# Stores on GpSimd's queue and a fourth staging tile in the wide part of a one-core decoder layer

## The chip, the cores and the metric

The kernel runs on one core of one Trainium2 chip. The metric is the device time of one execution in microseconds (us). A difference below 0.3%, about 6 us, can't be told from none with this kernel.

## The reference

One layer of a hybrid decoder on 1024 tokens of width 2048, all in float32. What matters here are its three large matrix products and what stands between them:

```python
h = rmsnorm(h_res, g_pre)
u = h @ w_in                      # 2048 x 7184: q, k, v, branch gates of both head groups
o_gla = rmsnorm(gla_chunked(...), g_gla_head) * silu(g_gate)
o_sb = stick_breaking(...) * silu(s_gate)
mix = concat([o_gla, o_sb]) @ w_out              # 2048 x 2048
h_res = h_res + rmsnorm(mix, g_post)
gate = sigmoid(h_res @ w_ple_gate + b_ple_gate)  # 2048 x 2048
out = h_res + gate * (p @ w_ple_proj)
```

## The kernel before

Everything is kept transposed: a tile has 128 features as its partitions and tokens along the free dimension. A wide tile is `[128, 1024]` float32, 512 KB, and holds two feature blocks for 512 tokens.

A float32 product is made of three matmuls in the rounded type fp32r. Each operand is split into a rounded part `hi` (an activation that copies, on ScalarE) and the rest `lo` (a subtraction on VectorE), both in `split`, L110. Then hi\*hi, lo\*hi and hi\*lo are added in PSUM. `product` (L866) does so for one column block of a weight and eight blocks of an activation: 24 matmuls of 128x512.

The first part (up to L807) is the projection `w_in` with the attention of both head groups beside it. The wide part, which the change touches, begins at L810. It computes the branch gates (`w_gate`, which are columns of `w_in`), `w_out` and `w_g`, each as a 2 x 2 block product with seven products instead of eight (Winograd's form). So each has a loop over eight columns j in which three quarters of the weight, `b11`, `t1` and `t2`, are loaded, subtracted from one another on VectorE and split, and two products are made per column: `S2` times `w2` and `S1` times `w1` (L1001 for the gates, L1062 for `w_out`, L1233 for `w_g`). In the first two, both `t2` and `b11` are stored to DRAM for later loops (`t2_d` and `t3_d`, which the trace calls `g_d`); in the third only `t2` is (`u_d`). The other loops load one or two weights per column.

What sets the order of the work:

- The tile framework's scheduler turns the program into one fixed order per engine, and a semaphore wait holds everything that stands behind it on that engine. `dma` and `dma2` (L65, L66) are both SP's `dma_start`, so all loads and stores of the kernel stand in SP's one order and go to one hardware queue.
- Weights are loaded into the four `wr` tiles (`wload2`, L853). A `wr` tile is free again when it is split, and, if it is stored, when the store has landed. Their splits go to three pairs `wh`, `wl`.
- Activations and intermediate results are loaded into three staging tiles `ar` (`staged`, L835). Jobs that run beside the loops (`fill`, `sums_12`, `stream`, `gates_11`) take these in turn, and make the split sets of activations for a later loop.
- `sums_12` (L909) is the job on which the first part of the prediction rests. For each of four blocks i it loads two blocks of `og_d` (the gated attention output) into staging tiles a and b, computes a = a + b and b = A11 - a, stores b to `s2_d` (in the trace `s_d`) and splits both. Its results are the sets `S1` and `S2` of the `w_out` loop with three weights (L1062). It runs beside the loop before that (L1051).
- Results are made in four wide tiles `ev`, in `st_u` and `st_v` (`st`), and for the last four columns of the first small products in two narrow tiles `cw` of `[128, 512]` (L818), each stored to `c11_d`.
- `to_slot` and `act_wide` hold the split activations (`ah`, `al`).

```python
def staged(src):
    t = mt("ar", 3)
    dma2(t, src)
    return t
```

GpSimd works in the first part only (sums of squares, masks, memsets).

Of the kernel before, what the change touches and what calls it, by code (L numbers as in the profile page):

```python
# [21 lines left out]
HT = 512  # L22
# [38 lines left out]
def layer(ctx, tc, xT, w_in, w_gate, w_lr, w_a2, b_a, g_pre, g_head, w_out, g_post,  # L61
          w_g, b_g, w_p, pT, ident, masks, sel_in, out):
    nc = tc.nc
    V, A, G, PE = nc.vector, nc.scalar, nc.gpsimd, nc.tensor
    dma = nc.sync.dma_start  # L65
    dma2 = nc.sync.dma_start  # L66
# [69 lines left out]
    def part(t, k):  # L136
        return t[:, (k % 2) * HT:(k % 2 + 1) * HT]
# [70 lines left out]
    x_act = {hf: [None] * KT for hf in HALVES}  # L208
# [59 lines left out]
    og_d = [[dram.tile([P, W], F32, name=f"og_d{n}_{hf}") for n in range(KP)] for hf in HALVES]  # L268

    keep = ctx.enter_context(tc.tile_pool(name="keep", bufs=1, reuse_waits="tile"))  # L270
    with tc.tile_pool(name="att", bufs=1, reuse_waits="tile") as ap:
# [483 lines left out]
        def small_product(a, src, evac):  # L755
            p = ps("dn")
            for q in range(2):
                hi, lo = wload(part(src, q))
                for kk in range(4):
                    k = 4 * q + kk  # L760
                    sl = slice(kk * P, (kk + 1) * P)
                    ah, al = a[k]
                    mm(p, hi[:, sl], ah, k == 0, False)
                    mm(p, lo[:, sl], ah, False, False)
                    mm(p, hi[:, sl], al, False, k == 7)
                    if k % 2:
                        step()
            with tc.high_priority(offset=300):
                evac(p)
# [15 lines left out]
        def keep_11(j, new):  # L785
            def go(p):
                t = new()
                V.tensor_tensor(t, p, part(u1_s[j // 2], j) if j < 6 else u1_s[j], op=ALU.add)
                dma2(part(c11_d[j // 2], j), t)
            return go  # L790
# [18 lines left out]

    mp = ctx.enter_context(tc.tile_pool(name="mix", bufs=1, reuse_waits="tile"))  # L810
    late = [None]

    def mt(tag, bufs, n=W, dt=F32, name=None):
        pool = keep if tag == "ar" else mp if tag in ("wr", "wh", "wl", "cw") else late[0]
        return pool.tile([P, n], dt, tag=tag, name=nm(name or tag), bufs=bufs)

    for j in order_11[8 - LAST_11:]:
        small_product(x_act[0][8:], w_gate[1, 0, j], keep_11(j, lambda: mt("cw", 2, HT)))  # L818
    w_open.__exit__(None, None, None)
    late[0] = ctx.enter_context(tc.tile_pool(name="late", bufs=1, reuse_waits="tile", side="right"))  # L820
    if True:
# [8 lines left out]
        def to_slot(s, i, raw):  # L830
            pair = act_wide(*slots[s][i])
            split(*pair, raw)
            return pair

        def staged(src):  # L835
            t = mt("ar", 3)
            dma2(t, src)
            return t

# [40 lines left out]
        st_u, st_v = state("h"), state("l")  # L880
# [28 lines left out]
        def sums_12():  # L909
            s1, s2 = [], []  # L910
            for i in range(4):
                a, b = staged(og_d[1][i]), staged(og_d[1][i + 4])
                add(a, a, b)
                hi, lo = sets["A11 pairs"][i]
                add(b, f(hi), f(lo))
                sub(b, b, a)
                dma2(s2_d[i], b)
                yield 1
                s2.append(to_slot(1, i, b))
                yield 1  # L920
                s1.append(to_slot(2, i, a))
                yield 1
            sets["S1"], sets["S2"] = parts(s1), parts(s2)
# [3 lines left out]
        m_d, s2_d, t2_d, t3_d = drams("m_d", 4), drams("s2_d", 4), drams("t2_d", 8), drams("t3_d", 8)  # L927
        c_d = [drams(f"c{hf}_d", KP) for hf in HALVES]
        h_d = [drams(f"h{hf}_d", KP) for hf in HALVES]
# [30 lines left out]
        def stream(hf, kp, c):  # L960
            x = staged(xT[hf, kp])
            for n in (2 * kp, 2 * kp + 1):
                V.scalar_tensor_tensor(part(c, n), part(c, n), gpost_s[:, n:n + 1], r[hf],
                                       op0=ALU.mult, op1=ALU.mult)
            add(c, c, x)
            dma2(h_d[hf][kp], c)
            yield 1


        wide = {}  # L970
# [12 lines left out]
        def finish(z, hf, kp):  # L983
            o, g = staged(o_d[hf][kp]), mt("sq", 1)
            z3 = z.rearrange("p (a t) -> p a t", a=2)
            V.tensor_tensor(z3, z3, rstd[hf].rearrange("p (o t) -> p o t", o=1).to_broadcast([P, 2, HT]),
                            op=ALU.mult)
            A.activation(g, z, AF.Sigmoid)
            V.tensor_tensor(z, z, o, op=ALU.mult)
            V.tensor_tensor(z, z, g, op=ALU.mult)  # L990
            dma2(og_d[hf][kp], z)

        def gates_11():
            for i in range(4):
# [4 lines left out]
        t2_d, t3_d = drams("g2_d", 8), drams("g3_d", 8)  # L999
        dma2(st_u[3], u1_d)  # L1000
        for j in range(8):  # L1001
            with ahead():
                b11, t1, t2 = (wload2(w_gate[kh, nh, j]) for kh, nh in ((0, 0), (0, 1), (1, 1)))
                sub(t1, t1, b11)
                sub(t2, t1, t2)
                w2, w1 = wsplit(t2), wsplit(t1)
                add(b11, b11, t2)
                dma2(t2_d[j], t2)
                dma2(t3_d[j], b11)
            p = product(g_sets["S2"], w2)  # L1010
            with soon():
                add(u(j), p, part(u1_s[j // 2], j) if j < 6 else u(j))
            p = product(g_sets["S1"], w1)
            with soon():
                add(v(j), p, u(j))
# [30 lines left out]
        st_u, st_v = state("h"), state("l")  # L1046
# [4 lines left out]
        for j in range(8):  # L1051
            with ahead():
                w = wsplit(wload2(w_out[0, 0, j]))
            p = product(sets["A11"], w)
            with soon():
                A.activation(u(j), p, AF.Copy)
                if j % 2:
                    dma2(m_d[j // 2], st_u[j // 2])
        drain()

        job(fill("S3", 0, both(og_d[1], og_d[0], sub)))
        for j in range(8):  # L1062
            with ahead():
                b11, t1, t2 = (wload2(w_out[kh, nh, j]) for kh, nh in ((0, 0), (0, 1), (1, 1)))
                sub(t1, t1, b11)
                sub(t2, t1, t2)
                w2, w1 = wsplit(t2), wsplit(t1)
                add(b11, b11, t2)
                dma2(t2_d[j], t2)
                dma2(t3_d[j], b11)  # L1070
            p = product(sets["S2"], w2)
            with soon():
                add(u(j), p, u(j))
            p = product(sets["S1"], w1)
            with soon():
                add(v(j), p, u(j))
# [4 lines left out]
        for j in range(8):  # L1081
            with ahead():
                w = wsplit(wload2(t3_d[j]))
            p = product(sets["S3"], w)
            with soon():
                if j % 2 == 0:
                    c = mt("ev", 4)
                add(part(c, j), p, v(j))
                add(u(j), p, u(j))
                if j % 2:  # L1090
                    dma2(c_d[1][4 + j // 2], c)
                    squares(1, c)
        drain()

# [25 lines left out]
        for j in range(8):  # L1120
            with ahead():
                w = wsplit(wload2(w_out[1, 0, j]))
            p = product(sets["A12"], w)
            with soon():
                if j % 2 == 0:
                    c = staged(m_d[j // 2])
                add(part(c, j), p, part(c, j))
                if j % 2:
                    dma2(c_d[0][j // 2], c)
                    squares(0, c)  # L1130
        drain()

# [38 lines left out]
        def gated(n, hf, p, other, last=False):  # L1171
            key = n // 8, hf
            if n % 2 == 0:
                wide[key] = mt("ev", 4)
                res[key] = staged(h_d[hf][n // 2])
            t, h = part(wide[key], n), res[key]
            add(t, p, other)
            g = mt("g", 1, HT)
            A.activation(g, t, AF.Sigmoid, bias=bg_s[:, n:n + 1])
            V.tensor_tensor(t, pw.pop((n, hf)), g, op=ALU.mult)  # L1180
            if last:
                add(t, t, part(h, n))
                dma2(part(out[hf, n // 2], n), t)
            elif n % 2:
                add(wide[key], wide[key], h)
                dma2(out[hf, n // 2], wide[key])

        def stream_0():
            norm(0)
# [43 lines left out]
        for j in range(8):  # L1233
            with ahead():
                b11, t1, t2 = (wload2(w_g[kh, nh, j]) for kh, nh in ((0, 0), (0, 1), (1, 1)))
                sub(t1, t1, b11)
                sub(t2, t1, t2)
                w2, w1 = wsplit(t2), wsplit(t1)
                dma2(t2_d[j], t2)
            p = product(sets["S2"], w2)  # L1240
            with soon():
                add(u(j), p, u(j))
            p = product(sets["S1"], w1)
            with soon():
                add(v(j), p, u(j))
# [99 lines left out]
```

## Time and profile before

| | us |
|---|---|
| median of three runs | 2112.08 |
| their range | 2111.71 to 2118.36 |
| the profiled execution | 2116.28 |
| its span, first to last instruction | 2114.6 |
| TensorE busy | 2078.6 (98%) |
| VectorE busy | 1502.2 (71%) |
| ScalarE busy | 873.9 (41%) |
| GpSimd busy | 106.6 (5%) |

In this profile a row of instructions names the source line, the engine, the operation and the tiles as out<-in. PE is TensorE, DVE is VectorE, ACT is ScalarE, POOL is GpSimd, SP is SyncE, and SPq is its queue, which issues the transfers. In a timeline row the first two numbers are the start and the duration in us; square brackets give the idle time before it and what ended that. The chain of waits has the same two numbers and then what filled the time. A landing is the time from the issue of a transfer to the semaphore that tells of its end. Matmuls are pipelined, so that the busy time of TensorE hides short losses.

### The profile page before, as it was taken

Reading aid. Unit: us, or ns where it says so; the run is one execution under the profiler, and the core shown is the slowest. Engines: PE = TensorE matmul, PEld = TensorE weight load, DVE = VectorE, ACT = ScalarE, POOL = GpSimd, SP = SyncE. Lnnn points to the kernel's source line nnn. Section 1 sums busy time; section 2 is a strip of 40 time slices with the busy share of each in tenths; the row PEclk is TensorE's granted clock in tenths of the full one; section 3 lists DMA queues with packets and bytes.
Section 4 is the critical chain, followed back from the end, with each engine's and each line's share of the span. In section 5 each row is a group of like instructions: output and inputs, shape, how many; then the busy total and the mean of one; then the engine's idle time right before and its main releaser. Section 6 shows DMA issues by size and latency. Waiting matters only on the chain.

```text
span 2114.6 us, 26802 instructions
## 1 busy us (share of the span) xinstructions
PE 2078.6 (98%) x9712; PEld 1709.8 (81%) x9712; DVE 1502.2 (71%) x2259; ACT 873.9 (41%) x1389; POOL 106.6 (5%) x228
## 2 busy tenths in 40 slices
PE   9999999999999999999999999999899999999998
PEld 6788888888887888888888787788688888777887
DVE  8557767676766676666567667897777787876665
ACT  7333433343455455545456313333233444423332
POOL 3000000000011011101101000000000000000000
PEclk9999999999999999999999999999899999999999
DMA  6222222222344344433335787887887685777763
GB/s 210 68 70 77 80 75 83 70 85 65 78 107 106 94 103 119 105 94 101 76 95 153 236 291 279 295 274 276 301 299 249 214 311 200 273 273 232 237 200 122
DMA packets 229812, 352.81 MB, mean 167 GB/s; under 512 B 124464, under 2 KB 129456, under 8 KB 229680
## 3 DMA queue, kind: packets, MB, share of 16 engines
q1 hardware_dynamic: 229680, 351.11, 52.7%
q8 instruction: 76, 1.25, 0.2%
q14 instruction: 56, 0.46, 0.1%
HBM read 249.85 MB, written 73.92 MB: 153 GB/s over the span
## 4 chain that ended last, share of the span: by engine, by line
PE 61%; DMA 16%; DVE 15%; issue 4%; ACT 3%; SPq 0%; POOL 0%; DVEq 0%; ACTq 0%; POOLq 0%
PE dn L100 52%; PE z L100 4%; DMA wr<-w_g 4%; DVE wl L112 3%; PE o L100 2%; PE t L100 2%; DMA wr<-w_gate 2%; DVE wr L848 1%; DMA E<-X 1%; DMA ar<-h_d 1%; DVE wr L851 1%; DVE ev L848 1%; DVE al L112 1%; DMA ar<-og_d 1%; DMA g_d<-wr 1%
## 5 line engine op out<-in xcount | busy, mean ns | idle before, releaser
L100 PE MATMUL dn<-ah,hi 128*128 128x512 f32 x1408 | 562.7, 400 | 2.0 <-ACT hi L111 1.3
L100 PE MATMUL dn<-al,hi 128*128 128x512 f32 x1408 | 550.7, 391 | 1.0 <-DVE al L241 1.0
L100 PE MATMUL dn<-ah,lo 128*128 128x512 f32 x1408 | 550.4, 391 | 0.2 <-DVE lo L112 0.2
L100 PE MATMUL dn<-ah,wh 128*128 128x512 f32 x1216 | 476.0, 391 | 7.8 <-ACT ah L111 5.5
L100 PE MATMUL dn<-ah,wl 128*128 128x512 f32 x1216 | 476.7, 392 | 5.4 <-DVE wl L112 5.3
L100 PE MATMUL dn<-al,wh 128*128 128x512 f32 x1216 | 474.9, 391 | 0.1
L100 PEld LDWEIGHTS dn<-ah,hi 128*128 128x128 f32 x1408 | 265.7, 189 | 61.5 <-ACT ah L240 4.2
L100 PEld LDWEIGHTS dn<-al,hi 128*128 128x128 f32 x1408 | 264.7, 188 | 59.9 <-DVE al L241 2.5
L100 PEld LDWEIGHTS dn<-ah,lo 128*128 128x128 f32 x1408 | 265.7, 189 | 48.3 <-DVE lo L112 0.5
L100 PEld LDWEIGHTS dn<-ah,wl 128*128 128x128 f32 x1216 | 229.4, 189 | 58.7 <-DVE wl L112 11.4
L100 PEld LDWEIGHTS dn<-ah,wh 128*128 128x128 f32 x1216 | 229.5, 189 | 57.9 <-ACT ah L111 6.5
L100 PEld LDWEIGHTS dn<-al,wh 128*128 128x128 f32 x1216 | 229.2, 188 | 47.9 <-DVE al L112 0.8
L111 ACT ACTIVATE wh<-wr 128x1024 fp32r<-128x1024 f32 x152 | 158.5, 1054 | 252.5 <-DVE wr L851 133.1
L112 DVE TENSOR_TENSOR wl<-wr,wh 128x1024 fp32r<-128x1024 f32 x152 | 184.9, 1218 | 6.4 <-ACT wh L111 6.0
L111 ACT ACTIVATE hi<-raw 128x512 fp32r<-128x512 f32 x192 | 120.1, 626 | 142.1 <-PE dn L100 136.3
L112 DVE TENSOR_TENSOR lo<-raw,hi 128x512 fp32r<-128x512 f32 x192 | 133.6, 697 | 57.9 <-ACT hi L111 57.5
L324 ACT ACTIVATE X<-E 128x256 uint16<-128x256 uint16 (+2 forms) x96 | 81.0, 843 | 127.0 <-DVE E L599 118.3
L594 DVE TENSOR_TENSOR_SCAN X<-X 128x128 f32<-128x128 f32 (+2 forms) x96 | 98.1, 1022 | 31.5 <-POOL X L588 21.6
L111 ACT ACTIVATE ah<-ar 128x1024 fp32r<-128x1024 f32 x56 | 59.2, 1060 | 121.3 <-DVE ar L848 63.8
L609 DVE COPY v<-E 128x512 uint16<-128x512 uint16 (+1 forms) x160 | 63.5, 428 | 55.1 <-DMA E<-X 45.7
L851 DVE TENSOR_TENSOR wr<-wr,wr 128x1024 f32<-128x1024 f32 x48 | 58.7, 1223 | 57.3 <-DMA wr<-w_gate 18.0
L848 DVE TENSOR_TENSOR wr<-wr,wr 128x1024 f32<-128x1024 f32 x48 | 58.8, 1224 | 50.9 <-DMA wr<-w_g 32.2
(233 smaller groups left out, 2305.7 us busy)
## 6 DMA issues: line engine op xcount, KB each, us to landing
raw<-w_in SPq DMA_DIRECT2D x160, 256.0 KB, 2.7
wr<-w_g SPq DMA_DIRECT2D x64, 512.0 KB, 4.3
wr<-w_out SPq DMA_DIRECT2D x56, 512.0 KB, 4.7
wr<-w_gate SPq DMA_DIRECT2D x40, 512.0 KB, 5.1
ar<-h_d SPq DMA_DIRECT2D x36, 512.0 KB, 4.9
g_d<-wr SPq DMA_DIRECT2D x32, 512.0 KB, 2.8
wr<-g_d SPq DMA_DIRECT2D x32, 512.0 KB, 4.6
ar<-og_d SPq DMA_DIRECT2D x32, 512.0 KB, 5.0
```

Of the source, the lines that this page charges most:

```text
L100: PE.matmul(o, lhsT, rhs, start=start, stop=stop)
L111: A.activation(hi, src, AF.Copy)
L112: (eng or V).tensor_tensor(lo, src, f(hi), op=ALU.subtract)
L324: A.activation(pl.rearrange("p (two n) -> p two n", two=2), src.bitcast(U16)[:, :2 * n].rearrange("p (n two) -> p two n", two=2), AF.Copy)
L594: V.tensor_tensor_scan(rev, rev, rev, initial=kq[:, n:n + 1], op0=ALU.mult, op1=ALU.bypass)
L609: V.tensor_copy(to[:, :, :m, j], w[:, :, 2 * g:2 * g + m])
L848: V.tensor_tensor(dst, a, b, op=ALU.add)
L851: V.tensor_tensor(dst, a, b, op=ALU.subtract)
```

## The change

All stores from the wide part on go through a new name, `store`, which is GpSimd's `dma_start`, except the last narrow ones to `out` (L1183). Loads stay on SP. The staging tiles become four: every fourth call of `staged` takes the wide tile `cw` in place of an `ar`. For that, the two narrow `cw` tiles of `[128, 512]` become one of `[128, 1024]`, which takes the results of columns j and j + 1 in its halves. The space for descriptors of transfers that GpSimd issues is doubled.

```diff
+    store = G.dma_start
...
+    cw = {}
+
+    def at_cw(j):
+        if j % 2 == 0:
+            cw[0] = mt("cw", 1)
+        return part(cw[0], j)
+
     for j in order_11[8 - LAST_11:]:
-        small_product(x_act[0][8:], w_gate[1, 0, j], keep_11(j, lambda: mt("cw", 2, HT)))
+        small_product(x_act[0][8:], w_gate[1, 0, j], keep_11(j, lambda: at_cw(j)))
...
+        spare = itertools.cycle((("ar", 3), ("ar", 3), ("ar", 3), ("cw", 1)))
+
         def staged(src):
-            t = mt("ar", 3)
+            t = mt(*next(spare))
             dma2(t, src)
             return t
...
-                dma2(s2_d[i], b)
+                store(s2_d[i], b)
...
-            dma2(h_d[hf][kp], c)
+            store(h_d[hf][kp], c)
...
-            dma2(og_d[hf][kp], z)
+            store(og_d[hf][kp], z)
...
-                dma2(t2_d[j], t2)
-                dma2(t3_d[j], b11)
+                store(t2_d[j], t2)
+                store(t3_d[j], b11)
...
-                    dma2(m_d[j // 2], st_u[j // 2])
+                    store(m_d[j // 2], st_u[j // 2])
...
-                    dma2(c_d[0][j // 2], c)
+                    store(c_d[0][j // 2], c)
...
-                dma2(out[hf, n // 2], wide[key])
+                store(out[hf, n // 2], wide[key])
...
-                   dynamic_dma_scratch_size=1024)
+                   dynamic_dma_scratch_size=2048)
```

The pair of stores of `t2` and `b11` occurs in the loops for the gates and for `w_out`, the one of `t2` alone in that for `w_g`; `c_d[1]` is stored in the same way as `c_d[0]`. Together 103 stores move from SP to GpSimd. The scheduler then orders anew. Up to the wide part no order changes.

**SP where the `w_out` loop with three weights begins.** In the program before, the loads for the fourth block of `sums_12` are the two of `og_d_1_712` and `og_d_1_716`. The names `wr` with numbers from 13627 on are the weights of the second and third column, and `g_d` and `m_d` are stores:

```order
L855 DMA wr_13698<-w_out 128x1024
L1069 DMA g_d_11584<-wr_13631 128x1024
L1070 DMA g_d_11592<-wr_13627 128x1024
L1058 DMA m_d_11530<-st_13191 128x1024
L855 DMA wr_13700<-w_out 128x1024
L855 DMA wr_13702<-w_out 128x1024
L837 DMA ar_13325<-og_d_1_712 128x1024
L837 DMA ar_13327<-og_d_1_716 128x1024
```

Now, still on SP, `wr_13518`, `wr_13520` and `wr_13522` are `b11`, `t1` and `t2` of the first column:

```order
L847 DMA ar_13282<-og_d_1_715 128x1024
L865 DMA wr_13518<-w_out 128x1024
L847 DMA ar_13323<-og_d_1_712 128x1024
L865 DMA wr_13520<-w_out 128x1024
L847 DMA cw_13325<-og_d_1_716 128x1024
L847 DMA ar_13541<-og_d_1_709 128x1024
L865 DMA wr_13522<-w_out 128x1024
```

The two loads have moved from behind the stores of the second column to between the weight loads of the first; one of them goes to `cw`, and no store stands among them. On VectorE the sums and splits of the fourth block, which stood behind the weights of the third column, now end next to the split of the first column's `t2`.

**TensorE at the same place.** In the program before, the first product with `S2` is `dn_13539`, and the first with `S1` is `dn_13583`:

```order
L100 MATMUL dn_13539<-ah_13296,wh_13528 128x512
L100 MATMUL dn_13539<-ah_13296,wl_13529 128x512
L100 MATMUL dn_13539<-al_13297,wh_13528 128x512
L100 MATMUL dn_13583<-ah_13230,wh_13532 128x512
L100 MATMUL dn_13583<-ah_13230,wl_13533 128x512
L100 MATMUL dn_13583<-al_13231,wh_13532 128x512
```

Now the product with `S2` is `dn_13537`, and `ah_13337` is its fourth pair:

```order
L100 MATMUL dn_13537<-ah_13294,wh_13526 128x512
L100 MATMUL dn_13537<-ah_13294,wl_13527 128x512
L100 MATMUL dn_13537<-al_13295,wh_13526 128x512
L100 MATMUL dn_13537<-ah_13337,wh_13526 128x512
L100 MATMUL dn_13537<-ah_13337,wl_13527 128x512
L100 MATMUL dn_13537<-al_13338,wh_13526 128x512
```

Before, TensorE left the product after its third pair, with 18 of 24 matmuls done, and began the next two in the same way; now each product runs through.

**SP and GpSimd in the gates' loop with three weights.** Before, on SP, with what each waits for (`DMAHWn` is one of eight semaphores that SP's transfers use in turn), one column:

```order
L1008 DMA g_d_11586<-wr_11817 128x1024 [waits DVE_49]
L1009 DMA g_d_11594<-wr_11813 128x1024 [waits DVE_49]
L855 DMA wr_11886<-w_gate 128x1024 [waits DMAHW6_49,DVE_49]
L855 DMA wr_11888<-w_gate 128x1024 [waits DMAHW1_49,DVE_49]
L855 DMA wr_11955<-w_gate 128x1024 [waits DMAHW7_49,DMAHW2_49]
```

Now the loads on SP (`DMASWn` are the eight semaphores of GpSimd's stores, in turn from 0), and a column's two stores on POOL:

```order
L865 DMA wr_11884<-w_gate 128x1024 [waits DMAHW1_49,DMASW6_49,DVE_49]
L865 DMA wr_11886<-w_gate 128x1024 [waits DMAHW2_49,DVE_49]
L865 DMA wr_11953<-w_gate 128x1024 [waits DMAHW3_49,DMASW7_49]
L865 DMA wr_11955<-w_gate 128x1024 [waits DMAHW4_49,DMASW0_49,DVE_49]
L847 DMA ar_12197<-S3x_d_748 128x1024 [waits DMAHW5_49,DVE_49]
L865 DMA wr_11957<-w_gate 128x1024 [waits DMAHW6_49,DMASW1_49]
```

```order
L1018 DMA g_d_11584<-wr_11815 128x1024 [waits DVE_49]
L1019 DMA g_d_11592<-wr_11811 128x1024 [waits DVE_49]
L1018 DMA g_d_11585<-wr_11886 128x1024 [waits DMASW0_49,DVE_49]
L1019 DMA g_d_11593<-wr_11882 128x1024 [waits DMASW1_49,DVE_49]
```

The stores have left SP's order, and its loads wait in place of them for the landing of the stores that GpSimd issues (`DMASW6` is that of `wr_11815`, `DMASW7` that of `wr_11811`).

More of the change, by code (lines that the diff above doesn't have):

```diff
@@ L1068, in layer @@
                 add(b11, b11, t2)
-                dma2(t2_d[j], t2)
-                dma2(t3_d[j], b11)
+                store(t2_d[j], t2)
+                store(t3_d[j], b11)
             p = product(sets["S2"], w2)
@@ L1090, in layer @@
                 if j % 2:
-                    dma2(c_d[1][4 + j // 2], c)
+                    store(c_d[1][4 + j // 2], c)
                     squares(1, c)
@@ L1238, in layer @@
                 w2, w1 = wsplit(t2), wsplit(t1)
-                dma2(t2_d[j], t2)
+                store(t2_d[j], t2)
             p = product(sets["S2"], w2)
```

## The prediction

> **What bounds the kernel now.** The page first:
>
> ```profile
> span 2114.6 us, 26802 instructions
> ...
> PE 2078.6 (98%) x9712; PEld 1709.8 (81%) x9712; DVE 1502.2 (71%) x2259; ACT 873.9 (41%) x1389; POOL 106.6 (5%) x228
> ```
>
> TensorE is the bound. But its busy time counts a matmul as 0.39 us although the next one starts sooner, so a busy share of 98% does not say how much is lost. The chain of waits gives the true pace, from a run with nothing in between:
>
> ```profile
> 1668.38 81.62 PE dn L100 x360
> ```
>
> 81.62 / 360 = 0.2267 us a matmul. A product of 24 therefore takes 5.44 us, and a column of two products 10.88. With this pace the table by stage (busy time and count of each engine, granted clock, DMA share, GB/s) tells what the wide part loses:
>
> ```profile
> 1208.00:1480.00 272.00, 270.92 (x1187) 221.64 (x1186) 214.10 (x210) 86.34 (x90) 0.00 (x0) 1.00 0.81 283
> 1480.00:1504.00 24.00, 15.38 (x40) 10.05 (x39) 13.69 (x12) 4.60 (x5) 0.00 (x0) 0.72 0.89 319
> 1504.00:1860.00 356.00, 354.39 (x1558) 291.51 (x1557) 278.88 (x298) 138.45 (x147) 0.00 (x0) 1.00 0.75 260
> 1860.00:1940.00 80.00, 76.43 (x333) 61.55 (x332) 59.37 (x60) 20.98 (x21) 0.00 (x0) 1.00 0.75 253
> ```
>
> Count times 0.2267, taken from the length: 2.9, 14.9, 2.8 and 4.5 us lost. So of some 25 us, 14.9 lie in 24 us, where the granted clock also falls to 0.72. All that this change can win lies in these four numbers; before 1195 us nothing moves. The waits of TensorE there:
>
> ```profile
> 1481.82 0.50 PE L100 MATMUL dn<-ah,wh 128*128 128x512 f32 x1 [1.05 <-ACT wh L111]
> ...
> 1494.20 0.80 PE L100 MATMUL dn<-ah,wh 128*128 128x512 f32 x1 [5.38 <-ACT ah L111]
> 1498.78 0.80 PE L100 MATMUL dn<-ah,wh 128*128 128x512 f32 x1 [1.21 <-ACT wh L111]
> ```
>
> The longest wait is for `ah`, a split activation: the last pair that `sums_12` makes. Followed back in the timeline:
>
> ```profile
> 1491.83 1.23 DVE L848 TENSOR_TENSOR ar<-ar,ar 128x1024 f32<-128x1024 f32 x1
> ...
> 1493.09 1.06 ACT L111 ACTIVATE ah<-ar 128x1024 fp32r<-128x1024 f32 x1 [10.84 <-DVE ar L848]
> ```
>
> The first sum of that pair starts only at 1491.83. SP's queue shows why its two staged loads are so late:
>
> ```profile
> 1480.62 0.33 SPq L1069 DMA_DIRECT2D g_d<-wr  x1
> 1481.88 0.33 SPq L1070 DMA_DIRECT2D g_d<-wr  x1
> 1482.28 0.43 SPq L1058 DMA_DIRECT2D m_d<-st  x1
> 1483.27 1.57 SPq L855 DMA_DIRECT2D wr<-w_out  x2
> 1484.88 0.94 SPq L837 DMA_DIRECT2D ar<-og_d  x2
> ```
>
> The two `ar` loads leave at 1484.88, behind three stores that had waited for their data and two weight loads queued behind these. Over the whole wide part SP waited for stores as follows (us in total, times, longest):
>
> ```profile
> SPq L1008 <- DVE wr L851: 42.5, 8, 6.0
> ...
> SPq L1069 <- DVE wr L851: 26.2, 8, 5.8
> ```
>
> **The change part by part.** *Stores to GpSimd.* 103 transfers leave SP. GpSimd is busy for 0.00 us in the table, so nothing stands in front of them there, and a store that waits for its data now holds up only other stores. What it costs is the landing. The trace shows no transfer issued by GpSimd, so I bound it by stores of SP (size, median us from issue to landing):
>
> ```profile
> g_d<-wr SPq DMA_DIRECT2D x32, 512.0 KB, 2.8
> ...
> u_d<-wr SPq DMA_DIRECT2D x8, 512.0 KB, 3.6
> ...
> c_d<-cw SPq DMA_DIRECT2D x4, 256.0 KB, 7.2
> ```
>
> The lower end is 2.8, or a little under since the loads of the own queue no longer stand ahead. The upper is 7.2, the slowest row. I take 3.6, the same kind of transfer under load, as the row nearest to a `g_d<-wr` that has some more work in front of it. The Trainium skill, "DMA: Bandwidth & Descriptors", section "Anatomy of one DMA — SWDGE (gpsimd) path", fits a GpSimd transfer as 2.0 us plus bytes over 436 GB/s; for 512 KB that is an estimate of 3.2 us, with which the sum would be the same.
>
> Who waits for a landing? In the two loops with three weights a column, the load of the next `t1` takes the buffer that the store of `t2` gives back. The chain in the first of them:
>
> ```profile
> 1238.36 2.58 DMA g_d<-wr
> ...
> 1241.00 1.51 DMA wr<-w_gate
> ...
> 1242.53 4.97 DMA wr<-w_gate
> ...
> 1247.59 1.24 DVE wr L851
> ```
>
> The store lands at 1240.94 and `t1` is loaded at 1241.00. But the next store hangs on `t2`'s load, which leaves at 1242.53 when VectorE has split the last weight. The next `t2` store leaves here:
>
> ```profile
> 1248.84 0.33 SPq L1008 DMA_DIRECT2D g_d<-wr  x1
> ```
>
> One round is 1248.84 - 1238.36 = 10.5 us against TensorE's 10.88. So a landing may be 1.53 us later before it delays `t2`, and 0.4 more before TensorE waits: 2.58 + 1.53 + 0.4 = 4.5 us. Up to there it costs nothing, beyond it each us costs one us a column, 14 times (seven in each of the two loops with two stores). At 3.6 this term is 0. In the third such loop, L1233, SP's longest waits from 1860 to 1940 are these, so its weight loads wait for VectorE rather than for a landing:
>
> ```profile
> SPq L855 <- DVE wl L112: 19.8, 14, 4.1
> ...
> SPq L1239 <- DVE wr L851: 9.6, 6, 3.3
> ```
>
> In the second loop the rounds were longer:
>
> ```profile
> 1513.18 0.33 SPq L1069 DMA_DIRECT2D g_d<-wr  x1
> ...
> 1558.08 0.33 SPq L1069 DMA_DIRECT2D g_d<-wr  x1
> ```
>
> Four rounds in 44.9 us, 11.2 each, with staged loads in between that now stand ahead of the loop's later columns. If it stayed so, 7 x 0.3 = 2 us would be lost.
>
> *The fourth staging tile and the new order.* The staged loads of the fourth pair stand ahead of the first column's `t1` and `t2` instead of behind the second's stores, and TensorE's order takes the pairs in turn. The stall of 14.9 us then needs another cause. The next one is VectorE: the fourth pair's five operations of 1.22 us, 6.1 us, must now be done before the products begin. Its idle time from 1438 to 1481 (busy, mean ns, then idle before and what ended it) is mostly in two rows:
>
> ```profile
> L851 DVE TENSOR_TENSOR wr<-wr,wr 128x1024 f32<-128x1024 f32 x4 | 4.9, 1222 | 2.1 <-DMA wr<-w_out 1.7 <-issue 0.4
> ...
> L848 DVE TENSOR_TENSOR ar<-ar,ar 128x1024 f32<-128x1024 f32 x2 | 2.5, 1225 | 6.5 <-DMA ar<-og_d 6.5
> ```
>
> 8.6 us idle take 6.1, with 2.5 to spare in 43. That is tight, so I charge 2 us, between nothing and the 6.1 of all five. It also covers the second loop's 2 us, which would fall on the same columns.
>
> *Narrow result tiles.* The sum for j = 4 writes a tile that the stores of j = 2 and 3 must have left. Those stores, and the sums (two each):
>
> ```profile
> 1198.80 1.36 SPq L789 DMA_DIRECT2D c_d<-cw  x2
> ```
>
> ```profile
> 1209.17 1.28 DVE L788 TENSOR_TENSOR cw<-dn,ar 128x512 f32<-128x512 f32 x2
> ```
>
> The later store leaves about 1199.6 and with 7.2 us lands at 1206.8, 2.4 before the sum. This costs 0; without that cover VectorE would stand for the difference once. The 1 KB more of descriptor space is taken from SBUF and lies on no path: 0.
>
> *The sum.* 14.9 gained, 2 charged, 0 for landings, 0 for the 10.2 us of small losses elsewhere: 12.9, say 13 us. From 1860 to 1940 the `t2` stores hold SP too (9.6 us), but its loads wait for VectorE twice as long; I leave these 4.5 us to the low end. The profiled execution took 2116.28 us (its span and 1.7 around it) and would take 2103.3; it lies 4.2 above the median of 2112.08, so against the median I give 2099.
>
> **The rivals.** *Slower: buffers come back later.* The `wr` buffers wait for GpSimd's landings, and 4.5 us is the point from which that decides. For it: the loops run at 10.5 against 10.88, so there is little slack, and the trace has a store row of 7.2. Against it: those stores stood behind four weight loads in their own queue. Price: 14 us for each us over 4.5. At 5.4 the gain is eaten (14 x 0.9 = 12.6). At 7.2 it is 14 x 2.7 = 38 lost against 12.9 won: 2137. From 5.9 on it is slower by over 0.3%. One way to get there is a clash with VectorE. If a store had to wait for the end of the running operation, 1.22 us at most by the rows here, it would land at 4.8 and cost 14 x 0.3 = 4 us; if it had to wait for several of them in a row, the price above holds. The Trainium skill speaks against this change: "SBUF — State Buffer", section "SBUF: two separate sides", says that GpSimd cannot write its descriptors while VectorE runs in a two-port mode. By the section "Who interferes with whom" tensor_tensor has no such mode, and all rows of VectorE quoted here are TENSOR_TENSOR; no run here yet shows the clash.
>
> *No change: the stall only moves.* The loads come early, but VectorE, with 2.5 us to spare, or the DMA engines (0.89 busy in the stall) deliver late all the same, and 10 to 15 us are lost in smaller pieces. For it: VectorE's spare time, and that three weights a column are loaded in the same 20 us. Against it: its 6.5 us of idleness ended with just the loads that now come earlier. It gives 2109 to 2114, about 2112. A rule of the Trainium skill would have it so, "DMA: Bandwidth & Descriptors", section "Issuing engines are not separate DMA queues": issuing from several engines saves only the time to issue. The stall's rows bear out something else, waiting in order ahead of the issue.
>
> **How the numbers follow.** I give the forecast 0.65, the slower rival 0.19, no change 0.16. About 0.3%, 6.3 us, is what a measurement can tell from no change. The forecast and what is around it (up to 2105) is faster, so faster is 0.65, same 0.16, slower 0.19. Low end: the 2 us not charged, and the 4.5 and the 2.8 us won as well, 2112.1 - 14.9 - 7.3 = 2090. High end: a landing of 5.9 us, 2118; this leaves out the slow rival's upper part (0.14) and some 0.04 below. The forecast's own range is 2090 to 2105.
>
> **What would show it.** Right: no wait over 1.5 us of TensorE at the start of the `w_out` loop of three weights, its clock at 1.00 there, `g_d<-wr` landing under 4.5 us from POOL, SP waiting for buffers alone. Wrong: weight splits (`wl`) as TensorE's longest waits, SP's `wr` loads ending their waits with `g_d` landings from POOL, and rounds of over 10.9 us in the loop near 1240; or the same loss near 1480 behind sums that start late with their loads long landed.

## The result: 1% slower

The changed kernel takes 2137.52 us (median of 6 runs, 2132.32 to 2143.46) against 2115.98 for the kernel before in the same session (6 runs, 2111.71 to 2124.56). The ratio is 1.010, with a 95% interval of 1.0073 to 1.0127: some 21 us slower, where the forecast was 13 us faster. That it lies near the 2137 of the slower rival is luck: the loss comes from other places, as will be seen. The profiled execution took 2136.08 us. Its page begins so:

```profile
span 2134.3 us, 26905 instructions
...
PE 2086.1 (98%) x9712; PEld 1713.8 (80%) x9712; DVE 1502.1 (70%) x2259; ACT 872.9 (41%) x1389; POOL 162.4 (8%) x331
```

TensorE does the same 9712 matmuls, VectorE and ScalarE the same work; GpSimd has 103 instructions more, 0.54 us each. The time is lost in waits. To see where, cut both traces at the same matmuls, counted from the first, and ask for the table by stage (length, busy time and count of each engine, granted clock, DMA share, GB/s). The kernel before:

```profile
1197.02:1363.65 166.63, 165.55 (x722) 134.30 (x720) 121.69 (x123) 44.97 (x46) 0.00 (x0) 1.00 0.81 288
1472.45:1515.07 42.62, 34.00 (x122) 25.48 (x120) 29.80 (x29) 11.14 (x12) 0.00 (x0) 0.84 0.82 289
1515.07:1583.07 68.00, 68.00 (x302) 56.31 (x300) 52.93 (x51) 24.72 (x24) 0.00 (x0) 1.00 0.86 307
1719.45:1858.30 138.85, 137.30 (x601) 112.16 (x600) 110.21 (x123) 57.74 (x68) 0.00 (x0) 1.00 0.75 257
```

The changed kernel, the same four stages:

```profile
1197.95:1372.39 174.44, 167.21 (x722) 134.10 (x720) 123.84 (x124) 46.33 (x47) 11.37 (x21) 1.00 0.81 286
1481.19:1515.01 33.82, 29.98 (x121) 23.51 (x120) 22.87 (x22) 8.74 (x9) 2.66 (x5) 0.95 0.94 349
1515.01:1586.77 71.76, 69.32 (x302) 56.02 (x300) 49.89 (x49) 22.35 (x22) 5.32 (x10) 1.00 0.73 258
1723.14:1879.61 156.47, 144.82 (x601) 116.93 (x600) 119.74 (x131) 59.57 (x71) 8.51 (x16) 0.95 0.73 246
```

The second number is the length. The gates' loop lost 7.8 us, the start of the `w_out` loop won 8.8, the rest of that loop lost 3.8, and the stage where the finishing of one half runs beside `w_g` lost 17.6. The stages between kept their length, the one from 1858 on won 2.5. The old stall at 1480 is gone (a wait of 5.4 us for `ah` before; the longest up to 1515 is now 1.7), but the granted clock there is 0.95 and not 1.00. I call the four stages gates, stall, `w_out` and finish below.

**Gates.** TensorE now waits for weight splits, and SP, where it waited for the stores' data, waits for their landing (us in total, times, longest). Two views of the changed kernel, TensorE and SP:

```profile
PE dn L100 <- DVE wl L112: 6.9, 8, 1.6
```

```profile
SPq L865 <- DMA g_d<-wr: 64.2, 13, 9.8
SPq L865 <- DVE wl L112: 21.0, 15, 4.1
SPq L847 <- DMA og_d<-ar: 16.8, 4, 7.5
```

64.2 us in place of 42.5 for the data. Half of the landings themselves are not much longer (x, KB, median us):

```profile
g_d<-wr POOLq DMA_DIRECT2D x16, 512.0 KB, 3.1
```

The slowest of these sixteen are the second column's two, 4.5 and 6.0 us. And each store starts later, too. VectorE's `t2` and GpSimd's store of it, in the changed kernel:

```profile
1227.80 2.48 DVE L861 TENSOR_TENSOR wr<-wr,wr 128x1024 f32<-128x1024 f32 x2 [4.43 <-issue]
...
1230.58 0.53 POOL L1018 DMA_DIRECT2D g_d<-wr  x1 [10.19 <-DVE wr L861]
```

The data were there at 1227.80 + 2.48 = 1230.28, GpSimd began 0.30 later. In the kernel before, VectorE was done at 1237.11 + 1.23 = 1238.34, and SP's store left at 1238.36:

```profile
1237.11 1.23 DVE L851 TENSOR_TENSOR wr<-wr,wr 128x1024 f32<-128x1024 f32 x1 [1.04 <-DMA wr<-w_gate]
```

**Finish.** Here the chain of waits of the changed kernel reads:

```profile
1799.98 8.09 DMA h_d<-ar
1808.08 4.98 DMA ar<-xT
...
1818.84 1.41 DVE ar L973 x2
1820.24 1.13 DVE al L112
1821.38 0.34 DVE pl L112
```

A store of `h_d` that GpSimd issued at 1799.98 takes 8.09 us to land; the load of `xT` into the same staging tile leaves at 1808.08. VectorE stands and waits for it:

```profile
1813.15 1.23 DVE L858 TENSOR_TENSOR ar<-ar,ar 128x1024 f32<-128x1024 f32 x1 [1.48 <-DMA ar<-xT]
```

Behind this sum, in the order of VectorE and ScalarE, stands the split of a small weight `pr`, which TensorE needs. After the wait TensorE is slow for a while:

```profile
1820.37 0.79 PE L100 MATMUL t<-ph,ph 128*128 128x512 f32 x1 [6.13 <-ACT ph L111]
...
1824.07 0.63 PE L100 MATMUL dn<-ah,wh 128*128 128x512 f32 x1
1824.49 0.63 PE L100 MATMUL dn<-ah,wl 128*128 128x512 f32 x1
...
1827.22 0.39 PE L100 MATMUL dn<-ah,wh 128*128 128x512 f32 x1
1827.45 0.39 PE L100 MATMUL dn<-ah,wl 128*128 128x512 f32 x1
```

From 1819.50 to 1826.30 the granted clock is 0.50, and matmuls start 0.42 or 0.43 us apart instead of 0.23. The same is seen from 1734.20 to 1741.00 and from 1860.50 to 1863.90, each time around the end of a wait. Of some 20 us that this stage takes beyond the pace of 0.2267 us a matmul, 13 are waits and 7 such slow matmuls.

The stores of this stage land later than SP's did (x, KB, median us from issue to landing), the kernel before and then the changed one:

```profile
h_d<-ar SPq DMA_DIRECT2D x7, 512.0 KB, 4.1
h_d<-st SPq DMA_DIRECT2D x4, 512.0 KB, 4.0
```

```profile
h_d<-ar POOLq DMA_DIRECT2D x7, 512.0 KB, 5.5
h_d<-st POOLq DMA_DIRECT2D x4, 512.0 KB, 7.0
```

### The profile page after: what moved, and what is told of

Read it like the earlier page. It is cut to its first block, busy times and chain, and to the rows that moved or that the text cites. A ratio compares the mean times of both kernels' runs of the same rounds, so it can differ in the third digit from the quotient of the medians.

```text
span 2134.3 us, 26905 instructions
## 1 busy us (share of the span) xinstructions
PE 2086.1 (98%) x9712; PEld 1713.8 (80%) x9712; DVE 1502.1 (70%) x2259; ACT 872.9 (41%) x1389; POOL 162.4 (8%) x331
## 5 line engine op out<-in xcount | busy, mean ns | idle before, releaser
L111 ACT ACTIVATE ah<-ar 128x1024 fp32r<-128x1024 f32 x46 | 48.6, 1061 | 109.5 <-DVE ar L861 41.3
```

What stands on the lines that cost most here:

```text
L111: A.activation(hi, src, AF.Copy)
```

## The experiments

Each is given with its ratio to the kernel before and the 95% interval; a thousandth is 2.1 us, and "us" behind it is the ratio's distance from 1 times 2114. Each was run 4 to 12 times. One caution holds for all: wherever a store moves, the scheduler also orders SP's loads and VectorE's work anew, so two kernels seldom differ in one thing only.

### Which part of the change

`tile_only` leaves every store on SP, `pool_only` leaves the three staging tiles and the narrow result tiles; `loops_sp` and `loops_pool` divide the 103 stores.

```diff
tile_only:   -    store = G.dma_start
             +    store = dma2
pool_only:   -            t = mt(*next(spare))
             +            t = mt("ar", 3)
             -        small_product(..., keep_11(j, lambda: at_cw(j)))
             +        small_product(..., keep_11(j, lambda: mt("cw", 2, HT)))
loops_sp:    g_d, u_d:  -store(...)  +dma2(...)
loops_pool:  s_d, h_d, og_d, m_d, c_d, out:  -store(...)  +dma2(...)
```

> Only the fourth staging tile; every store stays on SP. Theory A (a buffer that a store frees comes back later when GpSimd issues the store: in the two loops with three weights 8.1 and 3.8 us, and 17.6 us between 1700 and 1865 us, while the new order gains 8.9 at 1480): all losses go, the gain at 1480 stays, so 5 to 9 us faster than before, no TensorE wait over 3 us between 1700 and 1865. Rival B (the ring of four staging tiles and the order that it makes lose the 17.6 us between 1700 and 1865): that loss stays, so 5 to 9 us slower than before.

Measured: 0.9952 (0.9936 to 0.9968), 10 us faster. Theory A, by a small margin over its range; B falls. The stages of this kernel's trace:

```profile
1197.19:1365.42 168.23, 165.43 (x721) 134.47 (x720) 120.98 (x121) 44.22 (x45) 0.00 (x0) 1.00 0.81 288
1474.22:1503.09 28.87, 27.79 (x122) 22.37 (x120) 19.20 (x19) 5.83 (x7) 0.00 (x0) 1.00 0.88 311
1503.09:1571.87 68.78, 68.37 (x301) 56.17 (x300) 56.73 (x56) 25.38 (x25) 0.00 (x0) 1.00 0.90 327
1708.27:1848.66 140.39, 137.56 (x601) 112.19 (x600) 118.98 (x131) 57.27 (x70) 0.00 (x0) 1.00 0.79 275
```

Stall and `w_out` together take 97.7 us for 110.6 before: 12.9 won. TensorE's longest wait in the whole wide part is 1.9 us.

> Only the stores on GpSimd, three staging tiles and the narrow tiles as before. Theory A: the losses of the loops (12) and of 1700 to 1865 (17.6) stay, so 15 to 30 us slower than before, depending on whether the staged loads for the w_out loop come ahead of its weights and the 8.9 at 1480 are gained. Rival B: the loss of 1700 to 1865 goes, so about 3 us slower (12 lost in the loops, 8.9 gained).

Measured: 1.0137 (1.0117 to 1.0157), 29 us slower, at the upper end of what A expected.

> The change with the stores of the loops with three weights (g_d and u_d, 40 of 103) back on SP. Theory A: rounds of the gates' loop back to about 10.5 us, the 12 us of the two loops gone and the rest kept, so 6 to 10 us slower than before. Rival C (the loops lose to staged loads that now run beside them, whoever issues the stores): rounds stay at 11 and over, 15 to 20 us slower than before. Rival B expects as A does here.

Measured: 1.0048 (1.0031 to 1.0064), 10 us slower, as A expected. But the rounds of the gates' loop did not return to A's 10.5 us: over seven they are 11.2, as C said, and the gates still take 173.0 us of the changed kernel's 174.4. So C falls by the time, but A's account of the gates falls too.

> The change with only the loops' stores (g_d and u_d, 40 of 103) on GpSimd and the other 63 back on SP. Theory A: the loops' 12 us stay lost, the 17.6 between 1700 and 1865 come back, 8.9 gained at 1480: 0 to 5 us slower than before. Rival B: the loss of 1700 to 1865 stays, 17 to 20 us slower than before.

Measured: 1.0043 (1.0028 to 1.0058), 9 us slower: more than A's 5, far from B's 17. So the stores, with the order that they bring, are what costs. Against `tile_only` the loops' 40 cost 19 us, the other 63 cost 20, and all 103 cost 31. In the gates the two groups do not add either: 6.7 us more by the first alone, 4.8 by the second, 6.2 by both.

Lengths of the four stages, from the start of the same matmul to the same:

| kernel | gates | stall | `w_out` | finish |
|---|---|---|---|---|
| before | 166.6 | 42.6 | 68.0 | 138.9 |
| changed | 174.4 | 33.8 | 71.8 | 156.5 |
| tile_only | 168.2 | 28.9 | 68.8 | 140.4 |
| loops_pool | 174.9 | 40.7 | 72.3 | 140.8 |
| loops_sp | 173.0 | 29.5 | 68.4 | 156.1 |
| act_loops | 170.2 | 38.6 | 71.1 | 139.1 |
| guard_loops | 175.1 | 36.3 | 75.3 | 142.0 |
| act_all | 170.2 | 37.3 | 68.5 | 157.9 |
| guard_all | 176.5 | 34.1 | 77.6 | 155.4 |
| guard_act_loops | 167.5 | 33.5 | 74.5 | 140.2 |
| hd_pool | 167.0 | 33.3 | 68.0 | 148.6 |
| rest_pool | 172.5 | 30.0 | 68.6 | 142.2 |
| loops_pool_wr5 | 177.0 | 28.9 | 76.9 | 140.4 |

Each length is of one execution. `hd_pool` has in the stall stage SP's transfers of `tile_only` in the same order, and none of them moved to GpSimd, and takes 33.3 us against 28.9; so a difference of some 4 us in one stage does not count by itself.

The loops' loss is not mostly in the gates: against `tile_only`, `loops_pool` and `act_loops` both lose most in the stall stage, 11.8 and 9.8 us. In `loops_pool` the first two stores of the `w_out` loop land last of all (x, KB, median us, from 1476 to 1486), and TensorE waits for split weights (from 1475 to 1520):

```profile
g_d<-wr POOLq DMA_DIRECT2D x2, 512.0 KB, 8.8
```

```profile
PE dn L100 <- ACT wh L111: 7.3, 2, 4.1
```

### Which of the other stores

Of `tile_only`, `hd_pool` puts only the 16 stores of `h_d` on GpSimd, `rest_pool` only s_d, og_d, m_d, c_d and out, and `out_pool`, run later, only the 15 of the wide results.

```diff
hd_pool:    h_d only:                     -dma2(...)  +G.dma_start(...)
rest_pool:  s_d, og_d, m_d, c_d, out:     -dma2(...)  +G.dma_start(...)
out_pool:   out only:                     -dma2(...)  +G.dma_start(...)
```

> Only the 16 h_d stores of the finishing stage on GpSimd, the other 87 on SP. If the loss between 1700 and 1865 us comes from the ring of staging tiles that these stores free (SP's waits for their landing were 24.1 us in the change, 5.9 in tile_only): 12 to 17 us slower than tile_only, 2 to 7 slower than before. If it comes from the other stores (og_d, c_d, m_d, out): as tile_only.

Measured: 0.9974 (0.9964 to 0.9985), 5 us slower than `tile_only`: between the two expectations.

> The 47 stores that are neither the loops' nor h_d (s_d, og_d, m_d, c_d and out) on GpSimd, the others on SP. If h_d carries the loss: 3 to 7 us slower than tile_only (the og_d stores' 5 us near 1350 stay), so 3 to 7 us faster than before. If not: 12 to 17 slower than tile_only.

Measured: 0.9994 (0.9982 to 1.0005), 9 us slower than `tile_only`, again between the two. Neither carries the 20 alone; 5 and 9 make 14, which the intervals do not clearly set apart from 20. In the trace, `hd_pool` lengthens the finish stage to 148.6 us. In `rest_pool` the gates take 172.5, where its `og_d` stores lie, 4.3 more than in `tile_only` and no more than one execution leaves open.

> As tile_only, with the 15 stores of the wide result tiles (out) on GpSimd: nothing is loaded again from them, and their buffers are refilled by VectorE and ScalarE, not by a load at the head of SP's queue. If stores cost only through loads that wait for their buffers: within 3 us of tile_only, 7 to 12 us faster than before. If every store off SP's queue costs its share of the 33 us (0.32 each): 4 to 6 us slower than tile_only.

Measured: 0.9962 (0.9948 to 0.9977), 2 us slower than `tile_only`, within the intervals of both. These stores landed in 5.7 us on average, against 3.8 in `tile_only`: for a store whose buffer no load waits for, 2 us more of landing cost little or nothing.

### Why a store off SP's queue costs

`act_loops` and `act_all` let ScalarE issue the stores, on a third queue. `loops_late` makes GpSimd's later. `guard_loops`, `guard_all` and `guard_act_loops` add a transfer of 64 bytes of the same tile on SP, so that SP waits for the tile's data again (`guard_act_loops` with ScalarE's store).

```diff
act_loops, act_all:  -    store = G.dma_start
                     +    store = A.dma_start
loops_late:          +        G.tensor_copy(idle, src[:, :256])
                              G.dma_start(dst, src)
guard_*:                      G.dma_start(dst, src)
                     +        dma2(dram.tile([1, 16], F32, name=nm("guard")), src[:1, :16])
```

> As loops_pool, but the loops' 40 stores (g_d and u_d) are issued by ScalarE, from a queue that is neither SP's nor GpSimd's. Theory A1 (it is GpSimd's own delay: its store starts 0.28 us after its data, SP's 0.02, and lands alone in 2.85 against 2.57): time goes back to that of tile_only, 8 to 12 us faster than before, stores landing alone in about 2.6. Theory A2 (it is leaving SP's order: loads are issued ahead of the store or beside it, and the next load then waits for a landing at the head of SP's queue): time stays near that of loops_pool, 5 to 12 us slower than before. A third possibility, ScalarE held up by waiting for VectorE, would show as waits of ACT at the stores' lines.

Measured: 0.9986 (0.9972 to 0.9999), 3 us faster: 7 us slower than `tile_only`, 12 faster than `loops_pool`. Between the two theories.

> As loops_pool, with a copy of 256 columns of the stored tile on GpSimd ahead of each of the 40 stores, so that each leaves later by the copy's time, some 0.3 to 0.8 us. Theory A1: every 0.3 us of a store's delay is worth as much as GpSimd's own 0.55 cost, so 10 us or more beyond loops_pool. Theory A2: the delay falls into time that SP waits at other points, at most 4 us beyond loops_pool.

Measured: 1.0085 (1.0065 to 1.0106), 18 us slower, 9 beyond `loops_pool`. The copy took 1.08 us, more than I had put:

```profile
L815 POOL COPY idle<-wr 128x256 f32<-128x256 f32 x40 | 43.2, 1080 | 735.1 <-DVE wr L866 677.2 <-DMA c_d<-cw 54.3 <-DVE wr L863 3.7
```

24 columns of 1.08 us are 26 us; 9 of them reach TensorE, 0.35 of each. On the whole that is less than A1 said. But in the gates' loop, where the copy ahead of the `t2` store took 1.39 us in seven of eight columns, the rounds grew from 11.6 to 12.8, nearly one for one.

> As loops_pool, and beside each of the 40 stores a transfer of 64 bytes of the same tile on SP, in about the place where the store stood, so that SP's later loads again wait for the tile's data while the 512 KB still go through GpSimd. Theory A2 (what is lost is SP's waiting for the store's data, which held later loads back): most of the 20 us between tile_only and loops_pool come back, 3 to 8 us faster than before. Theory A1 (GpSimd's own delay, or a buffer's late return): nothing comes back, since buffers return no earlier, 8 to 14 us slower than before.

Measured: 1.0015 (1.0001 to 1.0028), 3 us slower: 6 of the 19 us came back. More than A1 said, far less than A2.

> As act_loops (the loops' 40 stores from ScalarE), with the 64-byte transfers of guard_loops on SP. Stores off SP's queue were seen to cost three ways: GpSimd's own start and landing (0.55 us), SP's lost waiting, and about 1.2 us more landing where two or more transfers are in flight, on either queue. If the third is small, this kernel is within 3 us of tile_only, 7 to 10 us faster than before. If it carries the loss, it stays near act_loops, 0 to 3 us faster than before.

Measured: 0.9967 (0.9955 to 0.9980), 7 us faster, 3 slower than `tile_only`.

With `loops_pool` these four make a square, here in us against `tile_only`:

| | SP does not wait | SP waits |
|---|---|---|
| stores by GpSimd | 19 | 13 |
| stores by ScalarE | 7 | 3 |

Taken as it stands, GpSimd in place of ScalarE costs 12 or 10, SP's lost waiting 6 or 4, and 3 are left for being on another queue at all (each figure to about 4 us, by the intervals). But the order differs as well: in the gates, of VectorE's 181 instructions in `loops_pool` and 179 in `act_loops`, 142 stand in the same sequence. So the square fits both theories in part and does not show either. By stage, GpSimd and ScalarE differ most in the gates (174.9 and 170.2, with the guard 175.1 and 167.5). What the guard changes in a stage stays near the 4 us that one execution leaves open. The loss of the stall stage is there with either issuer.

> The change with all 103 stores issued by ScalarE. Theory A2: SP's order is left here too, so 8 to 20 us slower than before, less than the change by what is GpSimd's own. Theory A1: as tile_only, 5 to 12 us faster. ScalarE's waits for the stored tiles would add to either.

Measured: 1.0073 (1.0054 to 1.0092), 15 us slower, as A2 said. But less `act_loops` it is 18 us for the other 63 stores, as much as the 20 with GpSimd; the finish stage is no shorter (157.9). There GpSimd's own delay is not needed for the loss.

> The whole change with such a 64-byte transfer on SP beside each of the 103 stores. Theory A2: the most of the 33 us between tile_only and the change come back, from 5 us faster to 4 us slower than before. Theory A1: as the change, 18 to 25 us slower than before, or more by the 103 issues of SP.

Measured: 1.0123 (1.0101 to 1.0144), 26 us slower, as A1 said and against A2. The finish stage stays at 155.4. So SP's lost waiting alone does not explain the finish stage either. The guard does not put everything back, though: a load of `h_d` that `tile_only` issues behind such a store leaves at 1803.00 here, ahead of the store at 1804.40, which lands in 7.00.

### Another buffer, and the descriptor space

`loops_pool_wr5`, `tile_wr5` and `change_wr5` have five weight buffers; `scratch_512` is their control.

```diff
*_wr5:         -        raw = mt("wr", 4)
               +        raw = mt("wr", 5)
*_wr5, scratch_512:  dynamic_dma_scratch_size=512
```

> As loops_pool, with five weight buffers for four (512 bytes of descriptor space make the room), so that a column's loads wait for a store that left one load earlier. If the loops lose because a buffer comes back late: 10 to 20 us faster than loops_pool, 2 to 10 us faster than before. If the loops lose because loads and stores in flight together slow one another: within 4 us of loops_pool, or slower, 5 to 15 us slower than before, since loads run further ahead.

Measured: 1.0032 (1.0016 to 1.0047), 7 us slower, only 2 less than `loops_pool`. By the profiles the stall stage is as short as in `tile_only` (28.9), but the gates (177.0) and the `w_out` loop (76.9) are longer by 8 each.

> As tile_only, with five weight buffers. If buffers that come back late still cost something there (rounds of the gates' loop at 11.4 us against TensorE's 10.88): 2 to 6 us faster than tile_only, 12 to 16 faster than before. If not: as tile_only, or a few us slower since the loads run further ahead.

Measured: 0.9938 (0.9919 to 0.9957), 13 us faster; not told apart from `tile_only`, though the gates' loop runs in rounds of (1274.97 - 1205.84) / 7 = 9.9 us from the first `t2` store to the eighth, for 11.4 in `tile_only`.

> The whole change with five weight buffers: the loss of the loops goes, that of the finishing stage, which has staging tiles and not weight buffers, stays: 10 to 20 us faster than the change, 2 to 12 us slower than before. If late buffers are not the loops' cause: as the change, 18 to 25 us slower than before.

Measured: 1.0140 (1.0119 to 1.0161), 30 us slower, worse than the change. I had expected 10 to 20 us back. With GpSimd's stores SP still waits 96.6 us for landings of `g_d` in `loops_pool_wr5` from 1190 to 1600 (134.0 in `loops_pool`, 20.4 in `tile_only`): the scheduler also puts the loads further ahead, so each still stands before a landing, with all others behind it. These runs therefore do not separate a late buffer from a full queue.

> The change with 512 bytes of descriptor space for 2048, every instruction in the same order. If the space does not matter: as the change, 18 to 25 us slower than before. If GpSimd has to wait for room in it: more, with longer stores of POOL.

Measured: 1.0101 (1.0080 to 1.0123), 21 us slower, as the change. The space is no cause.

## Why the prediction was wrong, step by step

**The stall: right for the tile.** 14.9 gained less 2 for VectorE was to be 12.9. With the stores left on SP the two stages of the `w_out` loop give just that, 110.6 - 97.7 = 12.9. The mechanism was the new order of the staged loads; the stores' leaving was not needed for it. In the changed kernel the same stages win only 110.6 - 105.6 = 5.0, and with the loops' stores alone off SP the stall stage takes 40.7 us (GpSimd) or 38.6 (ScalarE) instead of 28.9.

**"0 for landings": this step failed.** The prediction took one landing, 3.6 us, for all 103 stores, and a threshold of 4.5 us: "Up to there it costs nothing". For six of the eight columns in the gates' loop the figure held. Their `t2` landed in 2.85 to 3.3 us, and the loop's rounds, 11.41 us over seven, are no longer than those of `tile_only` (11.43), whose stores are on SP. So the prediction's sign of being wrong, rounds of over 10.9, came in the faster kernel as well.

What failed is one figure for every place. A store that leaves among other transfers lands much later. In the changed kernel the second column's pair in the gates took 4.5 and 6.0 us, and of the first three columns of the `w_out` loop the `b11` stores took 6.5, 4.6 and 7.3; the working had priced `t2`'s landing alone. In `loops_pool` the first two pairs of the `w_out` loop took 7.0 to 8.9. The loops' 40 stores cost 19 us, by the profiles 11.8 in the stall stage, 6.7 in the gates and 3.5 (less than counts by itself) in the rest of the `w_out` loop. By the prediction's own price, one us for each us beyond 4.5, the `t2` landings of `loops_pool` give only some 8 (my estimate: 1.5 + 4.2 + 2.5). So the price is short as well, and what fills the difference was not shown. `act_loops` and `guard_act_loops` show that it depends on who issues and on SP's waiting, or on the order that comes with them.

The slack was mis-sized too. I took one round of 10.5 us; over seven rounds, from the kernel before:

```profile
1205.73 0.32 SPq L1008 DMA_DIRECT2D g_d<-wr  x1
...
1281.49 0.33 SPq L1008 DMA_DIRECT2D g_d<-wr  x1
```

(1281.49 - 1205.73) / 7 = 10.82 against TensorE's 10.88: 0.06 us and not 0.4.

**The other 63 stores were not costed: the larger omission.** "0 for landings" stood for all 103, but the working looked at the loops alone. There the 3.6 us that I took were near the median of 3.1. The stores of `h_d` land in 5.5 to 7.0 us in the finish stage, with staging tiles behind them that the next load wants at once, and the 63 cost 20 us: 17.6 us of the changed kernel's loss lie in the finish stage. Their rows, and the loads behind them, were in the trace of before. Nor was the clock in the price of a wait: in the finish stage 7 us of slow matmuls came on top of 13 of waits.

**The rivals.** The slower one had the right sign, and the right words ("buffers come back later"), but not the right price: 14 us for each us beyond 4.5 would have given nothing at landings of 3.1. The clash with VectorE is not seen: GpSimd's issues took 0.53 us in all rows above, beside VectorE's TENSOR_TENSOR. "The stall only moves" did not happen in `tile_only`. With the loops' stores alone off SP most of the stall's length came back, and the second of the rival's reasons, transfers that deliver late, is in part borne out by landings of up to 8.9 us there.

"The stall only moves" had a rule beside it, of the Trainium skill, "DMA: Bandwidth & Descriptors", section "Issuing engines are not separate DMA queues": issuing from several engines saves only the time to issue. By it the stores alone would have made no difference; they cost 29 us (`pool_only`), so for this case the rule leaves something out.

**What stays open** is the finish stage. Shown is that GpSimd's or ScalarE's queue lengthens it alike (156.5 and 157.9), that SP's waiting does not bring it back, that `h_d` alone makes some 8 of the 16 us (148.6 against 140.4). One `h_d` store in `tile_only`, with the loads behind it on SP:

```profile
1775.79 0.33 SPq L976 DMA_DIRECT2D h_d<-ar  x1
1776.20 0.38 SPq L847 DMA_DIRECT2D ar<-h_d  x1
...
1778.61 0.38 SPq L847 DMA_DIRECT2D ar<-c_d  x1
1779.54 0.33 SPq L847 DMA_DIRECT2D ar<-xT  x1
```

The same store in `hd_pool`, SP's loads and then GpSimd's issue:

```profile
1779.21 0.33 SPq L847 DMA_DIRECT2D ar<-h_d  x1
1780.35 0.33 SPq L847 DMA_DIRECT2D ar<-c_d  x1
...
1787.84 0.33 SPq L847 DMA_DIRECT2D ar<-xT  x1
```

```profile
1780.62 0.53 POOL L976 DMA_DIRECT2D h_d<-ar  x1 [5.33 <-DVE ar L858]
```

On SP the store goes ahead of two loads and lands in 3.74 us; on GpSimd's queue both loads have left before it, and it lands in 7.21. The load of `xT` waits for the landing both times. A cause that fits, and is only argued, is the landing among other transfers. From each transfer's issue and landing after 1190 us I counted how many others of 256 KB or more were in flight when a store of 512 KB left, and took the mean landing (in brackets the number of stores):

| in flight | SP, tile_only | GpSimd, changed | ScalarE, act_all |
|---|---|---|---|
| 0 | 2.69 (11) | 3.09 (14) | 2.66 (13) |
| 1 | 3.28 (34) | 3.49 (27) | 3.15 (23) |
| 2 | 4.06 (34) | 5.31 (29) | 5.35 (29) |
| 3 | 5.47 (19) | 6.13 (24) | 6.15 (25) |

In these three kernels a store behind two transfers lands 1.2 to 1.3 us later off SP's queue. That is not so everywhere: in `act_loops` such stores of ScalarE take 3.24 (3) and those of SP 4.64 (23), and in the kernel before SP's take 4.49 (36). The rows mix kinds of store. For `h_d` alone the mean is 5.0 us in `tile_only` with 2.4 others in flight, and 6.6 in `hd_pool` with 3.2. So the later place, behind loads that used to follow, fits, but so does a new order: of VectorE's 174 instructions in the finish stage of `tile_only` and 185 in `act_all`, 120 stand in the same sequence. No run here moved the stores of a loop or of `h_d` and kept the order.

## What to carry to other kernels

Before taking a store off the loads' queue, list for each kind of store the load that wants its buffer, and price the landing by the slowest places, here the starts of the loops and the finish stage (5 to 9 us), and not by the median of a group (3.1). A store's place in the loads' queue may be worth something by itself: here its wait for the data held later loads back, and a transfer of 64 bytes in its place gave back 4 to 6 us, the new order included. And try the parts of a change apart: one gave 10 us and the other took 29. `tile_only`, with the fourth staging tile alone, is faster than both kernels (0.9952 of the time before); with a fifth weight buffer besides (0.9938) it is no slower.

## What the runs showed of the hardware

- A store of 512 KB that waits for its data leaves 0.02 us after them from SP and 0.28 to 0.30 us after them from GpSimd; with no other transfer of 64 KB or more in flight the quickest landed in 2.58 us from SP and from ScalarE, 2.84 from GpSimd.
- Transfers from different queues hardly overtook one another: in the changed kernel, of the transfers that left after one of GpSimd's 103 stores, on average 0.02 landed sooner.
- A copy of 128 x 256 floats took GpSimd 1.08 us on average, 1.39 for the first of a pair in the gates' loop.
- Around the end of three waits of TensorE in the changed kernel the granted clock was 0.50 for 3.4 or 6.8 us, and matmuls started 0.43 us apart instead of 0.23.
- GpSimd's issue of a store took 0.53 us, and 512 bytes of descriptor space made the change no slower than 2048 (1.0101 and 1.0100).
